# Output stages of a two-layer encoder trunk: another order of loads, additions and accumulators, and one gated row in steps

## The chip, the cores and the metric

The kernel runs on one core of a Trainium2 chip. A core has five engines, each of which works through its own list of instructions in order: TensorE (PE, the matrix multiplies, with its weight loads shown as PEld), VectorE (DVE), ScalarE (ACT), GpSimd (POOL) and SyncE (SP), which here only issues transfers (DMA). TensorE writes its sums into eight PSUM banks of 128 x 512 floats; everything else lives in SBUF tiles or in memory. The metric is the device time of one execution in microseconds (us).

## The reference

Inputs are x (1024 tokens x 1024 channels), 256 memory tokens and the weights of two layers. In each layer a normalised x goes through one wide input projection, several attentions work on its parts, their outputs are put side by side to 1536 channels, multiplied by a SiLU gate, and go through one output projection, which is added to x:

```
for l in range(DEPTH):
    h = rmsnorm(x, norm_gain[l])
    ...
    if l % 2 == 0:
        qa, ka, va, qb, kb, vb, qm, gate = split_cols(h @ w_in_even[e], SPLIT_EVEN)
        ...
        ya = global_gqa(...)
        yb = window_gqa(..., sink_b[e], rel_bias)
        ym = memory_attn(...)
        y = jnp.concatenate([ya, yb, ym], axis=-1) * jax.nn.silu(gate)
        x = x + y @ w_out_even[e]
    else:
        qc, kc, vc, qm, gate = split_cols(h @ w_in_odd[o], SPLIT_ODD)
        yc = neighborhood_attn(..., rpb_c[o])
        ym = memory_attn(...)
        y = jnp.concatenate([yc, ym], axis=-1) * jax.nn.silu(gate)
        x = x + y @ w_out_odd[o]
return rmsnorm(x, final_norm_gain)
```

The change concerns the lines `x = x + y @ w_out` of both layers and the gating of the last windowed heads of layer 0.

## The kernel before, in words

**Precision.** Every float32 operand of a product is split into a high part (rounded to the type that TensorE takes) and a low part (the rest). ACT makes the high part with a copy (L117), DVE or POOL the low part with a subtraction (L121 for operands, L1233 for weights). A product of two such operands is three matmuls: high by high, high by low, low by high.

**Who sets the order.** The program is written as if one instruction followed another. A planner then simulates the engines and gives every engine its own fixed list: of the instructions whose inputs and buffers it thinks ready, the one that comes first in the program goes first. `self.ahead(kind)` moves a group forward in that ranking by so many instructions (`AHEAD`, L35: in `out0` only the weights, `w`, by 300; in `out1` only `sink`, by 150). `issue_after(ins)` puts those instructions of a block that run on the engine of `ins` behind it. On the chip the lists are fixed: an instruction whose input is late holds up all that stand behind it on its engine. A tile's tag names a small set of buffers, which are used again as soon as the last reader of the old content is done; a load into a buffer still in use waits on SP.

**Layer 0 before its output stage.** `even` (L1824) runs four pairs of windowed heads, `window_pair` (L657), each in four groups g of 256 queries: scores on PE into `sa` banks, exponentials on ACT, scaling of the probabilities P on POOL (L702), transposes on PE (L125), their split on ACT and DVE (L526, L527), the product with the values on PE (L722) into the bank `pv`, and the close of the group (ACT copies half of `pv` to `bt`, DVE adds, L732). PE's waits in there are filled with other work from a list, `self.waiting`, of which `pull` takes some steps at given places: in the last pair (j = 3) these are the gates of rows 6 and 7 and the beginning of the output product (`begin_out`, L1240). When the gate of row 6 is complete, `gated_rows` writes all of its gating into the program at that one place (`gated`, L490): one multiply of 128 x 1024 on DVE (L499), a store of the result, a load of the partner row's halves back from memory, three subtractions of 128 x 512 on POOL (L510, L511, L513) and two more stores (L512, L514). Row 7, which needs the last group's result, follows after the pair (L1875).

**The output stage** (`out_project`, L1263) multiplies 12 row blocks of 128 gated channels. It is cut into two halves of channels, of tokens and of outputs, and uses seven half-size products in place of eight: a11, then t1 by s1, t2 by s2, t3 by s3, y22 by s4, y21 by a12 and t4 by a22. The t are sums and differences of the gated halves that the gating above stores in `yd`; the s are sums of weight blocks that `weight_sums` stores in `sd`. The channel blocks lie in the order `ROWS` (L44), so that row 6 is number 10 and row 7 number 11, the last one of a product. Each product has four output blocks i, each of 6 channel blocks x 3 = 18 matmuls of 128 x 512 (L1285), and takes two units of weights per block (192 KB each, loaded to `wraw`, split to `wh` and `wl`; four buffers of each). `y_parts` (L1176) loads the six operand blocks of a product (256 KB each, L1190) and splits them. A product's sum lies in a bank: `xb[i]` for a11 and, on top of it, t2 and t3; `yb[i]` for t1 and, on top of it, y22. `residual` (L1290) loads a block of x (256 KB, L1291) into the output tiles c11, c22, c12, c21, and `plus` (L1293, runs at L1294) adds a bank to it on DVE. `OUT` (L46) lists the tags of the operand and output tiles.

Before, the first two products stand in the program as: for each i the product a11, the load of c11's residual and the addition; then the six operand loads of t1; then for each i the weights of s1, the product, the load of c22's residual and the addition. In layer 0 the four `yb` banks are `tr[0]`, `pv`, `sa[0]` and `sa[1]`'s second halves, in this order; `pv` is the bank that the last windowed group still fills.

In layer 1 (`odd`, L1878; `near`, L1049) the gating already runs in steps, through `gated_steps` (L459), taken one at a time behind the scaling on POOL.

## Time and profile before

| what | us |
|---|---|
| median of 3 runs | 1513.12 |
| lowest and highest of them | 1510.55, 1514.97 |
| the profiled execution, its own time | 1518.44 |
| its span, first to last instruction | 1516.7 |
| PE busy in it | 1480.2 |
| granted TensorE clock, mean | 0.993 |

All times of the trace are us from the span's start. In a row of the timeline stand the start, the duration, the engine, the line, the operation, output<-inputs, the shapes, how many instructions were merged, and in brackets the idle time of the engine just before and what ended it. "SPq" is the issue of a transfer, not the transfer itself. A row of the waits reads: engine, tile and line that waited, what it waited for, the sum in us, how many times, the longest. In the view by windows, each engine's busy time is followed by the number of its instructions; then come the granted clock, the share of the DMA engines and their GB/s.

Layer 0's output stage runs from about 660 to 790 us of the span, layer 1's from about 1393 us to the end.

### The profile page before, as it was taken

The page shows a single profiled execution, that of the slowest core. Times are in us where ns is not written, and L with a number is a line of the kernel's source. Part 1 is how long each engine was busy: PE and PEld are TensorE (multiplying, and loading weights), DVE is VectorE, ACT ScalarE, POOL GpSimd, SP SyncE. Part 2 cuts the span into 40 slices and gives each one's busy share as a digit, 9 for nine tenths or more (in the row PEclk, how much of TensorE's full clock was granted, in tenths as well). Part 3 has the DMA queues.
Part 4 walks back from the last instruction along what each step waited for, and adds up shares of the span by engine and source line. Part 5 has one row for each costly group of instructions (what it writes and reads, how often), then busy time and mean ns, then how long its engine had stood idle before and what let it go on. Part 6 is the DMA issues. An engine that isn't in the chain of part 4 may idle for free.

```text
span 1516.7 us, 25292 instructions
## 1 busy us (share of the span) xinstructions
PE 1480.2 (98%) x8377; PEld 1272.6 (84%) x8377; DVE 1042.7 (69%) x2117; ACT 840.5 (55%) x1855; POOL 642.5 (42%) x766
## 2 busy tenths in 40 slices
PE   8999999999999999999999999999999999999997
PEld 8898897888888788887879877888898888888886
DVE  7686776777776667777577676654346777788754
ACT  7643664566656456655444444444346777778443
POOL 1323557746675645553450000002324555654455
PEclk9999999999999999999999999999999999999998
DMA  8956334334343524388653344567755577688833
GB/s 292 290 162 182 95 116 156 113 128 124 128 142 97 176 75 143 99 275 276 193 179 125 121 138 137 160 167 265 273 178 174 178 231 228 211 285 314 294 117 137
DMA packets 173859, 271.90 MB, mean 179 GB/s; under 512 B 15648, under 2 KB 96800, under 8 KB 172704
## 3 DMA queue, kind: packets, MB, share of 16 engines
q1 hardware_dynamic: 173296, 270.20, 55.2%
q8 instruction: 66, 1.08, 0.3%
q14 instruction: 65, 0.53, 0.1%
q10 hardware_dynamic: 432, 0.09, 0.0%
HBM read 174.28 MB, written 83.89 MB: 170 GB/s over the span
## 4 chain that ended last, share of the span: by engine, by line
PE 46%; DVE 4%; DMA 3%; issue 1%; ACT 1%; POOL 1%; SPq 0%; POOLq 0%; DVEq 0%; ACTq 0%
PE pj L62 10%; PE x L1532 6%; PE pj L1285 3%; PE pv L62 3%; PE y L1532 3%; PE sa L1285 3%; PE s L62 3%; PE s L1285 2%; PE tr L62 2%; PE tr L1285 2%; PE pv L1532 2%; PE pv L1285 2%; PE y L404 2%; PE pv L404 2%; DMA v<-vt 1%
## 5 line engine op out<-in xcount | busy, mean ns | idle before, releaser
L117 ACT ACTIVATE ph<-tr 128x512 fp32r<-128x512 f32 (+2 forms) x336 | 180.9, 540 | 123.1 <-PE tr L125 82.3
L527 DVE TENSOR_TENSOR pl<-tr,ph 128x512 fp32r<-128x512 f32 (+2 forms) x336 | 205.5, 614 | 55.2 <-ACT ph L117 54.2
L231 PE MATMUL pj<-H,wh 128*128 128x512 f32 x704 | 235.4, 414 | 0.5 <-DVE vt L302 0.2
L147 POOL TENSOR_SCALAR wh<-wraw 128x512 fp32r<-128x512 f32 x48 | 31.8, 665 | 271.3 <-PE x L1532 236.6
L117 ACT ACTIVATE wh<-wraw 128x384 fp32r<-128x384 f32 (+1 forms) x163 | 89.2, 553 | 102.4 <-PE tr L1285 13.5
L231 PE MATMUL pj<-H,wl 128*128 128x512 f32 x352 | 139.6, 397 | 0.0
L231 PEld LDWEIGHTS pj<-H,wh 128*128 128x128 f32 x704 | 120.6, 190 | 18.8 <-POOL wl L149 0.6
L62 PE MATMUL pj<-H,wh 128*128 128x512 f32 x384 | 121.4, 397 | 0.0
L125 PE MATMUL tr<-ident,P 128*128 128x128 f32 x752 | 117.5, 273 | 3.8 <-POOL P L702 1.3
L1084 POOL TENSOR_SCALAR pn<-pn,st 128x384 f32<-128x384 f32 (+1 forms) x128 | 75.2, 588 | 99.7 <-DVE st L1083 60.8
L1233 POOL TENSOR_TENSOR wl<-wraw,wh 128x384 fp32r<-128x384 f32 x56 | 64.1, 1146 | 114.4 <-ACT wh L117 80.4
L125 PEld LDWEIGHTS tr<-ident,P 128*128 128x128 f32 x752 | 89.1, 140 | 13.9 <-POOL P L702 2.6
L1005 ACT ACTIVATE P<-sa,st 128x1024 f32<-128x1024 f32 x64 | 71.6, 1118 | 45.2 <-DVE st L1004 25.4
L1082 ACT ACTIVATE pn<-pn,st 128x384 f32<-128x384 f32 (+1 forms) x128 | 75.1, 587 | 35.4 <-DVE st L1079 33.0
L1007 POOL TENSOR_SCALAR P<-P,st 128x1024 f32<-128x1024 f32 x64 | 74.3, 1164 | 33.7 <-DVE st L1006 28.9
L1004 DVE TENSOR_REDUCE st<-sa 128x1 f32<-128x1024 f32 x64 | 77.6, 1218 | 14.2 <-PE sa L1000 11.3
L62 PE MATMUL s<-k,q 128*128 128x384 f32 (+1 forms) x352 | 86.4, 341 | 0.0
L149 POOL TENSOR_TENSOR wl<-wraw,wh 128x512 fp32r<-128x512 f32 x52 | 68.2, 1313 | 27.0 <-ACT wh L117 24.1
L231 PEld LDWEIGHTS pj<-H,wl 128*128 128x128 f32 x352 | 66.4, 189 | 15.2
L62 PE MATMUL pj<-H,wl 128*128 128x512 f32 x192 | 75.8, 395 | 0.0
L821 PE MATMUL pj<-ah,H 128*128 128x256 f32 x384 | 72.5, 287 | 1.4 <-DVE H L766 1.3
L62 PEld LDWEIGHTS pj<-H,wh 128*128 128x128 f32 x384 | 66.7, 189 | 5.5
(503 smaller groups left out, 4200.6 us busy)
## 6 DMA issues: line engine op xcount, KB each, us to landing
wraw<-w_o SPq DMA_DIRECT2D x52, 256.0 KB, 3.9
y<-yb SPq DMA_DIRECT2D x24, 512.0 KB, 3.3
wraw<-s SPq DMA_DIRECT2D x64, 192.0 KB, 3.3
wraw<-w_e SPq DMA_DIRECT2D x44, 256.0 KB, 3.3
k<-k SPq DMA_DIRECT2D x42, 256.0 KB, 4.3
s<-bias SPq DMA_DIRECT2D x56, 192.0 KB, 2.0
y<-sg SPq DMA_DIRECT2D x20, 512.0 KB, 3.9
wq<-w_o SPq DMA_DIRECT2D x40, 256.0 KB, 3.6
```

Of the source, the lines that this page charges most:

```text
L62: return lambda *a, **k: self.tc.keep_in_program_order(getattr(self.engine, name)(*a, **k))
L117: return self.nc.scalar.activation(out, in_, AF.Copy, scale=scale)
L125: self.turned = self.fence = self.pe.transpose(o, i, self.ident)
L231: self.pe.matmul(a[:, :n], s[:, kt % UNIT, :], m, start=(kt == 0 and i == 0), stop=(kt == KT - 1 and i == 2))
L527: self.low = nc.vector.tensor_tensor(pl[:, :n], tr[:, :n], ph[:, :n], op=OP.subtract)
L821: self.last = nc.tensor.matmul(a[:, b * 256:(b + 1) * 256], x[kt][:, t], w, start=(kt + b + i == 0), stop=(kt == KT - 1 and i == 2), skip_ ...
L1004: nc.vector.tensor_reduce(st[:, 0:1], s, axis=AX.X, op=OP.max, negate=True)
L1007: self.normal = nc.gpsimd.tensor_scalar(pt, pt, st[:, 2:3], 0.5, op0=OP.mult, op1=OP.mult)
L1082: nc.scalar.activation(o, o, AF.Exp, bias=st[:, 0:1], scale=-1.0, accum_out=st[:, 2:3])
L1084: normal = nc.gpsimd.tensor_scalar(o, o, st[:, 3:4], 0.5, op0=OP.mult, op1=OP.mult)
L1285: last = nc.tensor.matmul(bank, s[:, k, :], y[3 * u + k][m][:, cols], start=start and u + k + e == 0, stop=u == 1 and k + e == 4, skip_gro ...
L1532: self.last = nc.tensor.matmul(bank, ws[s][:, k, :], b[k][m], start=start and k + i == 0, stop=k == UNIT - 1 and i == 2, skip_group_check= ...
```

## The change

Four edits in one:

1. In `out_project` the four a11 products stand alone. Behind them come the two weight units of s1 for i = 0, then t1's operand loads, with the weights of i = 1 put in ahead of the fifth of the six (`between`), then for each i the t1 product, and only then the residual load and addition of c11 and those of c22. This holds for both layers.
2. In layer 0 the `yb` banks come in the order `tr[0]`, `sa[0]`, `sa[1]`, `pv`.
3. Row 6 of layer 0 is gated through `gated_steps` instead of `gated_rows`: the multiply in two halves of 512, and the POOL subtractions and stores as steps.
4. `window_pair` takes one step (`later_job`) at each transposing round, its POOL part behind the group's last scaling; what is left over is taken after the pair.

```
@@ out_project
             if i >= begun:
                 with self.tc.issue_after(self.hold.ins) if self.hold else nullcontext():
                     product(first, xb[i], weights(i, "a11") if i > begun else self.early, True)
+
+        ready = [list(weights(0, "s1"))]
+        y = self.y_parts(yd, tags["y"][1], "t1", lambda: ready.append(list(weights(1, "s1"))))
+        for i in range(4):
+            product(y, yb[i], weights(i, "s1") if i > 1 else ready[i], True)
             residual(at(c11, i), i, 1)
             with self.ahead("sink"):
                 plus(at(c11, i), xb[i])
-
-        y = self.y_parts(yd, tags["y"][1], "t1")
-        for i in range(4):
-            product(y, yb[i], weights(i, "s1"), True)
             residual(at(c22, i), 4 + i, 2)
             with self.ahead("sink"):
                 plus(at(c22, i), yb[i])
@@ y_parts
-    def y_parts(self, yd, tags, kind):
+    def y_parts(self, yd, tags, kind, between=None):
...
+            if k == 4 and between:
+                between()
@@ build, layer 0
-                y = [tr[0], self.ps("pv"), sa[0][:, 1, :], sa[1][:, 1, :]]
+                y = [tr[0], sa[0][:, 1, :], sa[1][:, 1, :], self.ps("pv")]
@@ even, j == 3
-                self.lazily(lambda: self.gate(w, E_G + 6), lambda sg: self.gated_rows(sg, 6, y6, yd))
+                self.later_jobs = deque()
+                self.lazily(lambda: self.gate(w, E_G + 6),
+                            lambda sg: self.later_jobs.append(self.gated_steps(sg, y6, yd, ROWS.index(6))))
@@ even, after the pairs
+        while self.later_jobs:
+            deque(self.later_jobs.popleft(), 0)
         self.gated_rows(sgs[0], 7, y, yd)
...
+    def later_job(self, normal):
+
+        if self.later_jobs:
+            with self.tc.issue_after(normal.ins):
+                if next(self.later_jobs[0], self) is self:
+                    self.later_jobs.popleft()
@@ window_pair
             for t in range(0, len(todo), 2):
+                self.later_job(normal)
```

More of the change, by code (lines that the diff above doesn't have):

```diff
@@ L84, in __init__ @@
         self.pe, self.ready, self.due = self.nc.tensor, {}, 0
+        self.later_jobs = ()
     def ahead(self, kind):
```

## The prediction

> **What bounds the kernel now.** I read the page first: who is busy, and how much of the span is left over.

> ```profile
> span 1516.7 us, 25292 instructions
> PE 1480.2 (98%) x8377; PEld 1272.6 (84%) x8377; DVE 1042.7 (69%) x2117; ACT 840.5 (55%) x1855; POOL 642.5 (42%) x766
> ```

> PE is busy for all but 36.5 us, and the change takes no matmul away. So it can gain no more than the idle time of PE in the stages that it reorders, and only where nothing later takes it back. Next I read the view by windows for both output stages, and kept the windows in which PE has idle time (the first PE figure is its busy time in 10 us):

> ```profile
> 650.00:660.00 10.00, 8.94 (x54) 7.56 (x53) 7.85 (x18) 5.57 (x14) 6.82 (x7) 1.00 0.98 353
> ...
> 680.00:690.00 10.00, 7.58 (x34) 5.76 (x33) 5.81 (x10) 4.58 (x9) 1.09 (x1) 1.00 0.77 261
> ...
> 710.00:720.00 10.00, 9.69 (x41) 7.14 (x40) 8.01 (x13) 7.40 (x15) 2.45 (x2) 1.00 0.89 325
> ...
> 790.00:800.00 10.00, 8.23 (x51) 6.73 (x49) 6.79 (x20) 3.80 (x7) 1.17 (x1) 1.00 0.81 267
> ...
> 1390.00:1400.00 10.00, 8.71 (x42) 6.78 (x40) 9.90 (x18) 9.95 (x21) 1.01 (x1) 1.00 0.70 237
> ```

> That is 1.06 + 2.42 + 0.31 + 1.77 + 1.29 = 6.9 us. The 1.77 at 790 us follow the last sums of squares, which no edit touches; 5.1 us are in reach. Last, PE's timeline, only the rows in which it stood idle, and the place where its next work lay:

> ```profile
> 656.81 1.11 PE L125 MATMUL tr<-ident,P 128*128 128x128 f32 x5 [0.94 <-POOL P L702]
> ...
> 684.64 0.28 PE L722 MATMUL pv<-pl,v 128*128 128x256 f32 x1
> 686.97 0.73 PE L1285 MATMUL sa<-q,wh 128*128 128x512 f32 x2 [2.05 <-ACT wh L117]
> 688.07 0.51 PE L1285 MATMUL sa<-q,wl 128*128 128x512 f32 x1 [0.36 <-DVE wl L1233]
> ...
> 719.58 0.50 PE L1285 MATMUL pj<-H,wl 128*128 128x512 f32 x1 [0.31 <-DVE wl L1233]
> ...
> 1392.88 0.44 PE L62 MATMUL pv<-pl,v 128*128 128x384 f32 x1 [1.15 <-DVE pl L527]
> ```

> **Row 6 in steps: 0.94 us.** The wait at 656.81 is for the scaling of a group's probabilities, and POOL's timeline says why that was late:

> ```profile
> 651.62 1.29 POOL L510 TENSOR_TENSOR sg<-yb,sg 128x512 f32<-128x512 f32 x1 [3.27 <-DMA sg<-y]
> 652.88 1.74 POOL L511 TENSOR_TENSOR sg<-yb,sg 128x512 f32<-128x512 f32 x1
> 654.58 1.31 POOL L513 TENSOR_TENSOR yb<-sg,yb 128x512 f32<-128x512 f32 x1
> 655.85 2.59 POOL L702 TENSOR_SCALAR P<-P,st 128x384 f32<-128x384 f32 x4
> ```

> POOL first waits 3.27 us for row 6's partner to come back from memory, then does the three subtractions (1.29 + 1.74 + 1.31 = 4.3), and the scaling stands behind them. Its reciprocal was done well before:

> ```profile
> 653.99 0.16 DVE L697 RECIPROCAL st<-st 128x4 f32<-128x4 f32 x1
> ```

> At 654.15 the scaling could have started, 1.70 us sooner. With seven steps, one for each of three transposing rounds in groups 1 to 3, the partner's load falls into group 1, the first two subtractions behind group 2's scaling, the third behind group 3's. Both waits leave that place, and 0.94 us of PE's idle time goes. What the steps add: two multiplies of 512 in place of one of 1024 on DVE, and nothing on SP (the same five transfers). The subtractions now run beside group 3's scaling, for which there is a row:

> ```profile
> 663.69 4.27 POOL L702 TENSOR_SCALAR P<-P,st 128x384 f32<-128x384 f32 x4
> ...
> 668.42 2.10 DVE L121 TENSOR_TENSOR k<-k 128x512 fp32r<-128x512 f32 x2
> ```

> The same four scalings took 4.27 us here against 2.59 above, while DVE split operands. The moved subtractions can cost up to that difference, 1.68 us, on group 3, or nothing. I take nothing, since PE has no idle row between 656.81 and 686.97: a11 covers it. Should the cover be gone, it is 1.68.

> [...]

> **The order of accumulators, and weights and operands first: 2.41 us.** Before the gap at 684.9 us PE has done 12 of the 18 matmuls of t1's block 0; the last 6 need operands in the tile v, which the windowed heads hold until PE's last `pv` matmul at 684.64. The next block in the program is block 1, but its bank is `pv`, closed only here:

> ```profile
> 687.46 0.59 ACT L117 ACTIVATE bt<-pv 64x512 f32<-64x512 f32 x1
> ...
> 688.54 0.84 DVE L732 TENSOR_TENSOR yb<-pv,bt 64x256 f32<-64x256 f32 x2
> ```

> So the list of PE has block 2 (`sa`) first, with weights that come last, and ACT holds them behind operands of y22, whose loads took 6 us:

> ```profile
> 679.27 0.52 ACT L117 ACTIVATE wh<-wraw 128x384 fp32r<-128x384 f32 x1 [2.17 <-PE tr L1285]
> 684.18 0.63 ACT L117 ACTIVATE q<-q 128x512 fp32r<-128x512 f32 x1 [4.39 <-DMA q<-y]
> 684.72 0.51 ACT L117 ACTIVATE wh<-wraw 128x384 fp32r<-128x384 f32 x1
> ...
> 686.41 0.51 ACT L117 ACTIVATE wh<-wraw 128x384 fp32r<-128x384 f32 x1
> ```

> The chain of waits gives what a matmul takes when nothing holds it, 8.40 / 36 = 0.233 us:

> ```profile
> 1393.60 8.40 PE s L1285 x36
> ```

> With `sa[0]` as block 1's bank nothing is open: its first unit of weights is the one split at 679.27, ready when PE gets there at 684.9; its 9 matmuls last until 687.0, and the second unit (684.72) is ready by then; the third (686.41) follows. So both waits, 2.05 + 0.36, go. If y22's operands still stand ahead of the second unit and come later, up to all 2.41 stays. I take 2.41, because the edit takes away the bank that forced block 2 forward. The 0.31 at 719.58 has the same kind of cause (a weight unit behind operands on ACT and DVE); I count it as gone, between 0 and 0.31.

> What the reordering moves: 4 residual loads and 4 additions of c11 go past t1's 6 operand loads and up to 8 weight units on SP, and past their splits on DVE. No instruction is added. The loads before (source line 1291 in layer 0; issue in ns, then us to landing):

> ```profile
> L1291 SPq DMA_DIRECT2D P<-xT x12: 327/368/493, 648.8 to 676.7; - x12
> ...
> DMA to landing us min/median/max: 2.8/5.1/6.3
> ```

> An addition must be done before t2 writes on the same bank (`xb`). t1's 72 matmuls, 16.8 us, lie between; the load, 5.1 at the median, and the addition, 0.69 (the row of 1391.06 below), are covered by them.

> **Layer 1: 0.60 us.** DVE's timeline ahead of 1392.88:

> ```profile
> 1391.06 0.69 DVE L1294 TENSOR_TENSOR H<-H,pj 128x512 f32<-128x512 f32 x1
> 1391.66 0.69 DVE L467 TENSOR_TENSOR yb<-yb,mk 128x512 f32<-128x512 f32 x1
> 1392.28 0.88 DVE L527 TENSOR_TENSOR pl<-tr,ph 128x384 fp32r<-128x384 f32 x2
> ```

> The addition to c11 stands ahead of the split that PE waits for. Moved behind t1's products it frees 0.60 us (1391.06 to 1391.66); the bounds are 0 (`sink` still pulls it 150 places forward) and 1.15. PE has no other wait in that stage before its end, so nothing more can be won there.

> **The sum.** 0.94 + 2.41 + 0.31 + 0.60 = 4.26 us. The profiled execution took 1518.44, so it would take 1514.2. It lay 5.3 above the median of the three runs; on the median's scale, 1513.12 - 4.26 = **1508.9 us**. A measurement of this kernel can tell about 0.3% (4.5 us) from no change; the forecast lies almost on that bound.

> **Rivals.**

> *Given back at row 11.* t2's last operand is row 7's gated block (number 11). Its store and PE's first matmul with it, the 16th of block 0:

> ```profile
> 700.10 0.38 SPq L512 DMA_DIRECT2D y<-sg  x1
> ...
> 710.38 0.69 DVE L121 TENSOR_TENSOR H<-H 128x512 fp32r<-128x512 f32 x1 [0.24 <-ACT H L117]
> ...
> 711.15 0.40 PE L1285 MATMUL pj<-H,wh 128*128 128x512 f32 x1
> ```

> Split until 711.07, used at 711.15: no slack. If PE comes 2.41 sooner and this chain doesn't, PE waits here. Against it: the chain begins with the close of `pv`, which itself stood behind y22's splits on ACT from 684.9 to 687.46 and may move up as much. Kept would be 0.94 + 0.60: 1511.6.

> *More than the sum.* A new plan also shifts the other stages, which hold 36.5 - 6.9 = 29.6 us of idle time. A tenth of that on top: 1513.12 - 4.26 - 3.0 = 1505.9. For it speaks that such waits are many and small; against it, that nothing there is edited.

> *Slower: residual loads in front of row 7.* Before, SP issues the residuals early, into a time when nothing waits:

> ```profile
> 648.84 3.07 SPq L1291 DMA_DIRECT2D P<-xT  x4
> ```

> After, 8 of them (c11 and c22) follow t1's operands in the program, the last two of which wait for v:

> ```profile
> 686.83 0.38 SPq L1190 DMA_DIRECT2D v<-y  x1
> ...
> 691.26 0.32 SPq L508 DMA_DIRECT2D y<-yb  x1
> ```

> If they land between these two rows, 8 x 0.262 MB = 2.1 MB stand ahead of row 7's store and its partner's load. At the 353 GB/s of the window 650 to 660 that is 5.9 us, and 8 issues of 0.37 us (368 ns above) are up to 3.0 more. Row 11 has no slack, so t2 waits for all of it, and of the sum only 0.94 + 0.60 stays: 1517.5 to 1520.5, 1519 in the middle. It decides from about 6 loads on. Against it: the planner lets a ready load go past one that waits for a buffer, as y22's loads did here.

> *It doesn't do what it says.* Weights already rank 300 places forward; with the same lists in the end, 1513.1.

> **How the numbers follow.** Forecast 0.40, its own range 1506 to 1511 (all 5.1 us in reach and one replanned wait below; the 2.41 half closed and 0.9 of the contention above); 0.26 of it beyond the bound, 0.14 within. More than the sum 0.17, faster. Given back 0.12 and unchanged 0.05, both within. Slower 0.26. So faster 0.43, the same 0.31, slower 0.26. The range reaches to the far ends of both side cases, 1502 (the larger gain, less another 4 us of replanned waits) to 1520.

> **What would show it.** Right: no PE row with an idle time of 2 us between 680 and 692; block 1 of t1 in `sa` directly behind block 0; no POOL subtraction ahead of group 2's scaling; the addition of c11 behind the last window split in layer 1. Wrong: PE idle at t2's 16th matmul (given back), or SP rows of L1291 between the v loads and L508 with a later L512 (slower). A difference that lies outside 650 to 800 and 1380 to 1400 us would make the account wrong even where the time fits.

## The result, and the profile after

The changed kernel took 1516.76 us in the median of its runs, the kernel before 1511.97 us beside it on the same chip: a ratio of 1.0028 with a 95% interval of 1.0017 to 1.0039. The prediction was 1508.9 us, a gain of 4.26; the change lost about 4.8. The profiled execution took 1519.19 us, and its page differs little from the one before: PE has 1481.1 us of work and stands idle for 36.3 us, where it was 1480.2 and 36.5. Of all the runs here, one, of the two-edit kernel in the third session below, took 1795.22 us at a clock of 0.75; it is left out of every figure.

```profile
span 1517.4 us, 25283 instructions
PE 1481.1 (98%) x8377; PEld 1271.7 (84%) x8377; DVE 1041.5 (69%) x2118; ACT 840.0 (55%) x1855; POOL 640.6 (42%) x766
```

So the idle time that the change was to remove is still there, in other places. PE's timeline of the changed kernel, with only the rows in which it stood idle at the places of the prediction, the row ahead of the largest and the row behind the last wait of t1:

```profile
636.55 0.44 PE L683 MATMUL sa<-k,q 128*128 128x384 f32 x1 [0.48 <-DVE st L687]
637.55 0.44 PE L683 MATMUL sa<-k,q 128*128 128x384 f32 x1 [0.40 <-DVE st L687]
...
687.12 0.40 PE L1289 MATMUL sa<-k,wl 128*128 128x512 f32 x1
689.32 0.86 PE L1289 MATMUL sa<-q,wh 128*128 128x512 f32 x2 [1.80 <-ACT wh L118]
690.52 0.80 PE L1289 MATMUL tr<-v,wh 128*128 128x512 f32 x1 [0.34 <-ACT v L118]
...
692.57 0.79 PE L1289 MATMUL sa<-q,wl 128*128 128x512 f32 x1 [0.83 <-DVE wl L1237]
693.16 1.05 PE L1289 MATMUL sa<-q,wh 128*128 128x512 f32 x2
...
1394.05 0.44 PE L62 MATMUL pv<-pl,v 128*128 128x384 f32 x1 [1.15 <-DVE pl L528]
```

The line numbers are 1 to 5 higher than before (L1289 was L1285, L118 was L117, L1237 was L1233, L528 was L527). The wait of 0.94 us for POOL at 656.81 has gone, but 0.48 + 0.40 = 0.88 us stand ahead of it. The wait of 2.05 + 0.36 = 2.41 us at 685 has become 1.80 + 0.34 + 0.83 = 2.97 us at 687 to 692.6. The 0.31 us at 719 has gone. The 1.15 us of layer 1 is as it was. Together 0.94 + 2.41 + 0.31 = 3.66 us became 3.85: +0.2.

That is no explanation of 4.8 us. The row at 693.16 points to something else: two matmuls took 1.05 us, where a pair of the same form takes 0.62 to 0.64 elsewhere. The view by windows, cut where the granted clock changes, says why (PE's busy time is the first figure behind the length, the granted clock the third from the end):

```profile
686.38:689.79 3.41, 1.61 (x7) 0.87 (x6) 3.04 (x5) 3.39 (x7) 0.00 (x0) 1.00 1.04 399
689.79:693.20 3.41, 2.25 (x6) 1.04 (x5) 3.41 (x6) 1.56 (x3) 1.14 (x1) 0.50 0.77 250
693.20:696.62 3.42, 3.42 (x10) 2.65 (x9) 1.65 (x3) 0.52 (x1) 1.86 (x2) 0.50 0.80 281
696.62:700.03 3.41, 3.41 (x17) 2.81 (x16) 2.90 (x3) 1.09 (x3) 2.23 (x2) 1.00 0.38 127
```

PE was idle for 3.41 - 1.61 = 1.80 us of the first window. In the next two its clock was 0.50, and in the last of those, busy throughout, it began 10 matmuls where the window behind it has 17. Cut in the same way, the execution before had its idle time at this place spread over two such windows, and no fall:

```profile
682.48:685.90 3.42, 2.43 (x11) 1.72 (x10) 0.69 (x1) 1.70 (x4) 0.60 (x1) 1.00 0.94 329
685.90:689.31 3.41, 1.98 (x7) 1.35 (x8) 3.39 (x6) 2.65 (x5) 0.49 (x1) 1.00 0.45 152
689.31:692.72 3.41, 3.41 (x16) 2.77 (x15) 3.38 (x5) 2.03 (x4) 1.73 (x1) 1.00 0.63 212
```

It had falls elsewhere, at 61, 150, 235 and 1099 us, each behind a wait of 1.1 to 2.9 us; the changed kernel's execution had them at 235 and 1099. So both profiled executions have four such stretches (both also end at half clock, behind 1508 and 1512 us, as every profile here does). Whether a given wait is followed by a fall differs from one profiled execution to another: the 1.83 us at 150 us stand in all 14 profiles here, with a fall behind them in six. The profiled execution of the kernel before, 1518.44 us, lay 6.5 us above that kernel's median, the changed one's 2.4 above its own. So two profiled spans, 1516.7 and 1517.4 us, can lie 0.7 us apart while the medians lie 4.8 apart.

### The profile page after: what moved, and what is told of

Read it like the earlier page. It is cut to its first block, busy times and chain, and to the rows that moved or that the text cites. A ratio compares the mean times of both kernels' runs of the same rounds, so it can differ in the third digit from the quotient of the medians.

```text
span 1517.4 us, 25283 instructions
## 1 busy us (share of the span) xinstructions
PE 1481.1 (98%) x8377; PEld 1271.7 (84%) x8377; DVE 1041.5 (69%) x2118; ACT 840.0 (55%) x1855; POOL 640.6 (42%) x766
## 4 chain that ended last, share of the span: by engine, by line
PE 78%; DMA 8%; DVE 6%; issue 3%; POOL 3%; ACT 2%; SPq 1%; POOLq 0%; DVEq 0%; ACTq 0%
PE pj L232 14%; PE pj L62 10%; PE x L1537 6%; PE tr L126 5%; PE pj L1289 4%; PE sa L1289 3%; PE pv L1034 3%; PE y L1537 3%; PE pv L62 3%; PE s L62 3%; PE s L1289 2%; PE tr L1289 2%; PE tr L62 2%; PE pv L1537 2%; PE sa L1001 2%
## 5 line engine op out<-in xcount | busy, mean ns | idle before, releaser
L118 ACT ACTIVATE ph<-tr 128x512 fp32r<-128x512 f32 (+2 forms) x336 | 180.9, 540 | 121.4 <-PE tr L126 80.1
L528 DVE TENSOR_TENSOR pl<-tr,ph 128x512 fp32r<-128x512 f32 (+2 forms) x336 | 205.5, 615 | 58.1 <-ACT ph L118 57.1
L118 ACT ACTIVATE wh<-wraw 128x384 fp32r<-128x384 f32 (+1 forms) x163 | 88.9, 552 | 97.1 <-PE pj L1289 12.8
L232 PEld LDWEIGHTS pj<-H,wh 128*128 128x128 f32 x704 | 120.1, 190 | 18.7 <-POOL wh L148 0.6
L62 PE MATMUL pj<-H,wh 128*128 128x512 f32 x384 | 121.4, 397 | 0.0
L126 PE MATMUL tr<-ident,P 128*128 128x128 f32 x752 | 116.5, 273 | 1.9 <-POOL P L641 1.2
L1237 POOL TENSOR_TENSOR wl<-wraw,wh 128x384 fp32r<-128x384 f32 x56 | 62.0, 1110 | 118.1 <-ACT wh L118 99.5
L126 PEld LDWEIGHTS tr<-ident,P 128*128 128x128 f32 x752 | 89.0, 140 | 11.3 <-POOL P L641 2.6
L62 PE MATMUL s<-k,q 128*128 128x384 f32 (+1 forms) x352 | 86.3, 341 | 0.0
L62 PE MATMUL pj<-H,wl 128*128 128x512 f32 x192 | 75.8, 395 | 0.0
L1237 DVE TENSOR_TENSOR wl<-wraw,wh 128x384 fp32r<-128x384 f32 (+1 forms) x67 | 51.3, 766 | 29.6 <-ACT wh L118 29.5
```

The source lines that it names most:

```text
L62: return lambda *a, **k: self.tc.keep_in_program_order(getattr(self.engine, name)(*a, **k))
L118: return self.nc.scalar.activation(out, in_, AF.Copy, scale=scale)
L126: self.turned = self.fence = self.pe.transpose(o, i, self.ident)
L232: self.pe.matmul(a[:, :n], s[:, kt % UNIT, :], m, start=(kt == 0 and i == 0), stop=(kt == KT - 1 and i == 2))
L528: self.low = nc.vector.tensor_tensor(pl[:, :n], tr[:, :n], ph[:, :n], op=OP.subtract)
L1237: engine.tensor_tensor(lf, raw, hf, op=OP.subtract)
```

## The experiments

Each run lists the mean granted clock, so a kernel's mean clock is the mean over its runs. The product of span and clock of a run is roughly its length at the full clock (roughly, because the product counts the clock also where TensorE stands idle). Over some 12 runs the difference of two such means is known to about 1.4 us; the changed kernel's third time has only 6 runs, and there it is about 2.5. "Clock" and "full-clock length" below are these two means, the latter as the difference to the kernel before in the same session. The kernel before ran in every session, the changed kernel in the second and third; "the steps" are edits 3 and 4.

| kernel | median us | ratio to before, 95% | clock (before's) | full-clock length |
|---|---|---|---|---|
| edit 1 undone | 1513.64 | 0.9998 [0.9982, 1.0014] | 0.9963 (0.9958) | +1.2 |
| edit 1 alone | 1514.78 | 1.0002 [0.9987, 1.0018] | 0.9959 (0.9958) | +0.4 |
| changed, y22's splits held | 1511.68 | 1.0004 [0.9983, 1.0025] | 0.9965 (0.9958) | +1.6 |
| before, y22's splits held | 1512.19 | 1.0004 [0.9987, 1.0020] | 0.9956 (0.9958) | 0.0 |
| changed, second time | 1515.13 | 1.0024 [1.0005, 1.0043] | 0.9941 (0.9958) | +0.4 |
| changed, wait filled | 1512.43 | 0.9998 [0.9988, 1.0009] | 0.9962 (0.9958) | +0.1 |
| edits 1 and 2 | 1512.29 | 0.9997 [0.9983, 1.0010] | 0.9955 (0.9958) | -1.3 |
| edit 1 and the steps | 1515.93 | 1.0019 [1.0003, 1.0034] | 0.9952 (0.9958) | +1.8 |
| changed, third time | 1517.97 | 1.0045 [1.0027, 1.0062] | 0.9937 (0.9960) | +2.3 |
| changed, filled elsewhere | 1516.47 | 1.0029 [1.0017, 1.0041] | 0.9945 (0.9960) | +1.9 |
| edits 1 and 2, second time | 1511.24 | 0.9999 [0.9986, 1.0011] | 0.9958 (0.9960) | -0.8 |
| edits 1 and 2, wait in t1 filled, seven matmuls more at 150 us | 1511.71 | 1.0005 [0.9994, 1.0016] | 0.9969 (0.9960) | +1.5 |

**First session: which part, and is it the operands of y22?** Theory A took the loss for edit 1's: the loads of y22 go out late, their splits hold the weights on ACT, PE waits and then has half its clock. Theory B put it on row 6 in steps, theory C on chance. The first kernel is the changed one with the order of the first two products as before, the second the kernel before with edit 1 alone.

> The changed kernel without its first edit (a11's additions, t1's operands and weights in the order of before), with the other order of accumulators and row 6 in steps. Theory A: the loss comes from the first edit, which sends residual loads just ahead of y22's operand loads; y22's splits then come late on ACT (first at 686.05 after 684.18) and hold the weights of t1's block 2, so PE idles 1.80 + 0.34 + 0.83 us at 687 to 693 and then runs 6.83 us at half clock. Then this kernel is not slower than before: ratio to before 0.998 to 1.000. Theory B: the loss comes from row 6 in steps (the last scores of the windowed heads lie at 660.8 instead of 659.4). Then it stays slow: ratio 1.002 to 1.004. Theory C: the clock falls by chance and the plan costs only 0.6 us more idle time: ratio about 1.000.

> The kernel before with the first edit alone (order of loads, weights and additions in both output stages; accumulators and row 6 as before). Theory A: about as slow as the whole change, ratio to before 1.002 to 1.004, with the wait for weights in t1 and the fall of the clock behind it. Theory B: no slower than before, 0.999 to 1.001. Theory C: about 1.000.

Edit 1 undone gave 0.9998 and edit 1 alone 1.0002. A expected 1.002 to 1.004 for edit 1 alone and fails as the account of the whole loss; B expected that for the kernel without edit 1 and fails too. Neither part has the loss by itself. C, chance, expected about 1.000 for both and isn't refuted by these runs.

In the other two kernels the splits of y22's operands in layer 0 may not be issued before the last weight split of s1, so nothing of y22 stands ahead of t1's weights:

```
-        self.copy(hf, raw)
-        engine.tensor_tensor(lf, raw, hf, op=OP.subtract)
+        self.w_last = self.copy(hf, raw), engine.tensor_tensor(lf, raw, hf, op=OP.subtract)
...
+        behind = self.w_last
...
+        held = self.held
+        if not last:
+            self.held = behind
         y = self.y_parts(yd, tags["y"][4], "y22")
+        self.held = held
```

> The changed kernel, with the splits of y22's operands in layer 0 put behind the last weight split of s1 on ACT and on the engine of its low part; nothing else is touched. Theory A: the weights of t1's block 2 are split at about 685, PE's waits in t1 go, and so does the half clock: ratio to before 0.996 to 0.999, to the changed kernel 0.993 to 0.997. Theory B: still slower than before, 1.001 to 1.003. Theory C: 0.6 to 3 us less than the changed kernel, 1.000 to 1.002 to before.

> The kernel before with the same hold on y22's splits. Theory A: the 2.05 + 0.36 us wait at 685 to 688 goes or shrinks to the wait for the weight buffer (under 1 us): ratio to before 0.997 to 1.000. If the wait in the kernel before comes from the bank of the last windowed group instead, it stays: 1.000.

The held kernel before gave 1.0004: no difference. In its profile the wait at 685 is gone, but one of 1.91 us stands at 697.56, with a fall behind it. The held changed kernel gave 1.0004 too. Its interval, up to 1.0025, still reaches the loss of 1.0024 to 1.0045 measured elsewhere, so that it is without the loss is likely and not shown; it gains nothing against the kernel before, where A had 0.996 to 0.999. Its profile was the surprise. PE's timeline has more waiting there than the changed kernel's 2.97 us:

```profile
685.24 0.50 PE L1288 MATMUL tr<-v,wh 128*128 128x512 f32 x1 [1.56 <-ACT v L118]
...
694.07 0.50 PE L1288 MATMUL pv<-k,wl 128*128 128x512 f32 x1 [1.20 <-POOL wl L1236]
...
698.31 0.50 PE L1288 MATMUL pj<-H,wl 128*128 128x512 f32 x1 [1.44 <-DVE wl L1236]
```

That is 4.2 us, but in three pieces some 4 to 9 us apart, and the clock did not fall. So the sum of the waits may not be what sets the time; how close together they lie might. From here theory H says: the changed kernel's wait in t1 is concentrated enough that TensorE's clock falls behind it in most executions, and that is the loss.

**Second session: the clock, by filling the wait.** The rivals were P (the plan itself is longer, at the same clock) and I (chance). The changed kernel ran again, and then with seven matmuls of t1's own operands put into the wait. They compute nothing that is kept.

```
             product(y, yb[i], weights(i, "s1") if i > 1 else ready[i], True)
+            if i == 1 and not last:
+                with self.tc.issue_after(self.mid.ins):
+                    for _ in range(7):
+                        nc.tensor.matmul(yb[i + 1], ready[i][0][0][:, 0, :], y[0][0], start=True, stop=True, skip_group_check=True)
```

(`self.mid` is the twelfth matmul of the block.)

> The changed kernel once more, beside before on the same chip. Theory H (half clock): the wait in t1 (layer 0) lies within about 5 us now (1.80 + 0.34 + 0.83 us), so that the granted clock falls there in most executions; the median ratio is 1.002 to 1.004, the mean granted clock of its runs is 0.001 to 0.003 below that of before's runs, and span times clock agrees with before's within 1 us. Theory P (the plan itself is longer, by waits and later work): 1.002 to 1.004 with the same mean clock, span times clock 3 us or more longer. Theory I (the difference was chance, or that chip's): 0.999 to 1.001.

> The changed kernel with seven matmuls of t1's own operands (0.234 us each, 1.64 us) issued behind block 1's first twelve matmuls in layer 0, into block 2's accumulator, which the block's first matmul overwrites: the wait stays as it is, but TensorE isn't idle in it. Theory H: the clock no longer falls near 690 us, the mean clock of its runs is 0.001 to 0.002 above that of the unfilled kernel on this chip, and the ratio to before is 0.998 to 1.001, that is 0.001 to 0.003 under the unfilled one. Theory P: as the unfilled kernel or slower, 1.002 to 1.005. Theory I: 0.999 to 1.002, as the unfilled one.

The changed kernel gave 1.0024 at a clock of 0.9941 against 0.9958, and the full-clock lengths lie 0.4 us apart. With that C falls as well. Filled, it gave 0.9998 at 0.9962. That is 2.7 us faster in the median, with seven matmuls more. H named both in advance; P and I fail. PE's timeline of the filled kernel shows that the wait is still there:

```profile
688.46 1.79 PE L1326 MATMUL sa<-q,wh 128*128 128x512 f32 x7
691.06 0.73 PE L1289 MATMUL sa<-q,wh 128*128 128x512 f32 x2 [0.81 <-ACT wh L118]
692.17 0.50 PE L1289 MATMUL tr<-v,wh 128*128 128x512 f32 x1 [0.38 <-ACT v L118]
...
693.50 0.50 PE L1289 MATMUL sa<-q,wl 128*128 128x512 f32 x1 [0.60 <-DVE wl L1237]
```

1.79 us of filling and 0.81 + 0.38 + 0.60 us of idle time make 3.58 us, no less than 2.97. But its windows have no idle time above 1.29 us, and the clock stays at 1.00:

```profile
687.33:690.75 3.42, 2.92 (x13) 2.04 (x11) 2.26 (x5) 2.95 (x6) 0.00 (x0) 1.00 1.06 402
690.75:694.16 3.41, 2.12 (x7) 1.17 (x8) 3.41 (x5) 2.42 (x5) 0.90 (x1) 1.00 0.71 239
694.16:697.57 3.41, 3.29 (x15) 2.39 (x14) 2.37 (x4) 0.53 (x1) 0.72 (x2) 1.00 0.94 334
```

The price can be read from the stage. From PE's last `pv` matmul of the windowed heads to its first matmul of t2 the filled execution took 702.55 - 682.77 = 19.78 us; the changed kernel's took 703.02 - 681.65 = 21.37 and 701.67 - 680.12 = 21.55, each with two stretches at half clock, and 700.79 - 680.17 = 20.62 in the third session, with one.

In the same session ran the changed kernel without the steps (edits 1 and 2 alone) and without the new accumulators (edit 1 and the steps):

> The changed order of the first output stage and of the accumulators, but row 6 gated as before. Theory H: the same wait in t1 as in the changed kernel, so 1.001 to 1.004 and a mean clock 0.001 to 0.002 under before's; if the wait falls apart into pieces under 1.5 us, 0.999 to 1.001 and before's clock. Theory P, row 6 in steps being the cost: 0.997 to 1.000; the two orders being the cost: 1.002 to 1.004 with the same clock. Theory I: 0.999 to 1.001.

> The changed order of the first output stage and row 6 in steps, accumulators as before. Theory H: the second product's block waits for the last window's two addends on pv in one piece of about 2 us (1.98 us in the kernel with the order alone), so the clock falls there in about half of the executions: 1.000 to 1.002, clock 0 to 0.001 under before's. Theory P, accumulators being the cost: 0.998 to 1.000; else 1.002 to 1.004. Theory I: 0.999 to 1.001.

Without the new accumulators, block 1 waits for `pv`'s bank and operands in one piece, and the kernel is slower, 1.0019, with a fall behind it. H had put the wait at 2 us and the ratio at 1.000 to 1.002. Of its 2.8 us in the mean, though, 1.8 are full-clock length and only 1.0 is clock:

```profile
685.64 0.70 PE L1289 MATMUL pv<-q,wh 128*128 128x512 f32 x2 [3.13 <-ACT k L118]
```

Without the steps there is no loss, 0.9997, as H allowed for a wait in pieces. Its PE rows at the two places:

```profile
652.90 1.11 PE L126 MATMUL tr<-ident,P 128*128 128x128 f32 x5 [0.82 <-POOL P L703]
...
683.50 0.40 PE L1289 MATMUL sa<-k,wl 128*128 128x512 f32 x1
683.74 0.73 PE L1289 MATMUL sa<-q,wh 128*128 128x512 f32 x2
684.83 0.50 PE L1289 MATMUL tr<-v,wh 128*128 128x512 f32 x1 [0.36 <-ACT v L118]
...
686.97 0.59 PE L1289 MATMUL sa<-q,wl 128*128 128x512 f32 x1 [1.42 <-DVE wl L1237]
```

Block 2's high weights are there when block 1's twelve matmuls end (683.50 + 0.23). The two orders without the steps have 0.36 + 1.42 = 1.78 us of waiting in t1, the changed kernel 2.97. The clock fell behind it in this profile too, for one stretch, and so it did at this place in the profiles of edit 1 alone (682.50) and of edits 1 and 2 the second time (684.56), which show no loss. So a fall in t1 is not the changed kernel's alone; what its profiles have and these don't is, in two of three, a second stretch. The wait of 2.05 us in the kernel before can be followed by a fall too, by the counts of the last section; one profile of a kernel can't tell how often.

**Third session: is it the place of the filling?** Theory F held that seven more matmuls anywhere re-plan the stage. The control puts the same seven ahead of block 1 of the sixth product (y21), behind t1; the order of the matmuls up to there is the changed kernel's.

```
             parts = list(weights(i, "a12"))
+            if i == 1 and not last:
+                for _ in range(7):
+                    nc.tensor.matmul(xb[i], parts[0][0][:, 0, :], y[0][0], start=True, stop=True, skip_group_check=True)
```

> The changed kernel a third time, as the reference of this call. Theory H (half clock): 1.001 to 1.004, mean clock 0.001 to 0.003 below before's; in the profile the wait in t1 of layer 0 leaves TensorE idle for more than 1.7 us of one stretch of 3.41 us and the granted clock falls to 0.50 behind it, for two stretches. Theory F (the filled kernel was faster because its schedule came out another way, not by the clock): the same ratio.

> The changed kernel with the same seven matmuls (0.234 us each, 1.64 us) issued ahead of the second block of the sixth product (y21, layer 0), some 80 us behind the wait in t1, into an accumulator that the block's first matmul overwrites; the order of all other matmuls is the changed kernel's. Theory H: the clock falls in t1 as in the changed kernel, and the seven matmuls cost up to 1.64 us: 1.002 to 1.005, clock 0.001 to 0.003 below before's. Theory F (seven matmuls more, anywhere, re-plan the stage): 0.999 to 1.001.

Filled elsewhere: 1.0029 at a clock of 0.9945 against 0.9960; the changed kernel beside it 1.0045 at 0.9937. F fails. The control's windows show the fall, two stretches again:

```profile
682.82:686.23 3.41, 0.90 (x4) 0.38 (x2) 2.49 (x5) 3.17 (x7) 0.00 (x0) 1.00 1.05 400
686.23:689.64 3.41, 2.48 (x5) 1.09 (x5) 3.41 (x5) 2.11 (x5) 1.17 (x1) 0.52 0.68 221
689.64:693.06 3.42, 3.42 (x8) 2.72 (x9) 1.67 (x3) 0.52 (x1) 1.31 (x2) 0.50 0.90 308
```

The last two kernels were to beat both: the two orders without the steps, and the same with the wait in t1 filled and with seven matmuls meant for a wait of 1.83 us ahead of layer 0's first scores, which all 14 profiles have.

```
+                if not self.filled:
+                    self.filled = True
+                    for _ in range(7):
+                        nc.tensor.matmul(s[:, 0:512], self.h[0][0][:, 0:128], self.h[0][0][:, 0:512], start=True, stop=True, skip_group_check=True)
                 for c in range(0, T, 512):
```

> The two changed orders without row 6 in steps, again, as the reference of the next kernel. Theory H: the wait in t1 in two pieces, 0.998 to 1.001, clock within 0.001 of before's. Theory F: the same.

> The two changed orders without row 6 in steps, with seven matmuls (0.234 us each) into the wait of t1 in layer 0, and seven of resident operands into the wait of 1.83 us ahead of layer 0's first scores (about 148 us), which all profiles so far show and behind which the clock fell in four of ten. Theory H: no stretch at half clock at 150 or 690 us, mean clock 0.001 to 0.002 above that of the two edits alone, 0.9975 to 1.0000: faster than both kernels, if by little. Theory F: 0.999 to 1.002, as the two edits alone or slower.

The clock rose as H expected, 0.9969 against 0.9958, and neither place fell in the profile. But the kernel gained nothing by it: 1.0005, against 0.9999 for the unfilled one. H's 0.9975 to 1.0000 is missed, and F's 0.999 to 1.002 holds. The trace says why this is no test of filling two waits. In t1 the filling took the whole wait: PE has no idle row there. At 150 us it did not:

```profile
149.54 1.89 PE L1003 MATMUL sa<-H 128*128 128x512 f32 x7 [1.83 <-DVE q L122]
```

The seven matmuls began behind the wait, which is as long as before, and added their own length. That the clock didn't fall there owes nothing to them: the grid of stretches (last section) happened to cut the idle time there into 0.31 and 1.52 us. So of the fourteen matmuls, 3.3 us at 0.234 us each, half are pure cost; the full-clock length is 2.3 us above the unfilled one's. No version beat the kernel before by more than the interval.

## Why the prediction was wrong

**Where the time went.** In the second session the changed kernel's mean time was 1516.07 us, 3.02 above that of before; 0.4 of this is full-clock length, 2.7 is clock. The clock is 0.0017 lower, which over 1517 us is 1517 x 0.0017 / 0.5 = 5.2 us more at half clock per execution, or 1.5 stretches of 3.41 us. The profiles show such stretches where the change works: all four of the unfilled kernel's schedule (three of the changed kernel, one of the control) have half clock in t1, three of them for two stretches; the one profile of the kernel before has none there. In the third session the full-clock length is 2.3 us longer as well (six runs; 1.9 in the control, 1.6 of whose matmuls were added). That is more than the +0.2 of the idle times, and this part stays open. The table hints at one cause: the kernels with the steps stand at +0.1 to +2.3 in the last column, those without, nothing added, at -1.3 to +0.4. So the steps may cost something beside the clock; no run was made to test it.

**The order of accumulators and weights first, 2.41: the step that failed.** "So both waits, 2.05 + 0.36, go" was half right. Block 1 does run in `sa` directly behind block 0, as foretold, but the next thing is late: block 2's weights. The prediction named this bound ("if y22's operands still stand ahead of the second unit and come later, up to all 2.41 stays") and took the other end: of the third unit of weights it says that it "follows", at no cost. It was split at 686.41 before and is split at 688.76 now, 1.41 us after PE had come to the end of what it could do (687.12 + 0.23). So 2.41 us of waiting did not go but became 2.97. SP and ACT of the changed kernel show it:

```profile
673.46 0.32 SPq L489 DMA_DIRECT2D y<-yb  x1
...
675.81 0.85 SPq L1295 DMA_DIRECT2D yb<-xT  x2
676.72 0.90 SPq L1295 DMA_DIRECT2D P<-xT  x2
...
679.34 0.91 SPq L1295 DMA_DIRECT2D P<-xT  x2
...
680.82 0.85 SPq L1194 DMA_DIRECT2D q<-y  x2
```

```profile
686.05 0.63 ACT L118 ACTIVATE q<-q 128x512 fp32r<-128x512 f32 x1 [4.33 <-DMA q<-y]
686.70 0.60 ACT L118 ACTIVATE bt<-pv 64x512 f32<-64x512 f32 x1
687.20 0.62 ACT L118 ACTIVATE q<-q 128x512 fp32r<-128x512 f32 x1
687.72 1.14 ACT L118 ACTIVATE k<-k 128x512 fp32r<-128x512 f32 x2
688.76 0.51 ACT L118 ACTIVATE wh<-wraw 128x384 fp32r<-128x384 f32 x1
```

ACT sat idle for 4.33 us in front of y22's first operand, with the weights behind it in its list. On DVE the low half came later still, behind the gating of row 7 and two more splits:

```profile
688.82 1.22 DVE L500 TENSOR_TENSOR yb<-yb,sg 128x1024 f32<-128x1024 f32 x1
689.95 1.29 DVE L122 TENSOR_TENSOR k<-k 128x512 fp32r<-128x512 f32 x2
691.16 1.35 DVE L1237 TENSOR_TENSOR wl<-wraw,wh 128x384 fp32r<-128x384 f32 x1
```

**Why the parts matter together.** The operand chain is what PE meets, and the steps move it. In the changed kernel y22's first load goes out at 680.82, 3.75 us before block 1 begins (684.57). In the kernel without the steps it goes out 6.67 us before (674.27 against 680.94), behind four residual loads and not six:

```profile
652.43 0.72 SPq L515 DMA_DIRECT2D y<-yb  x1
...
658.49 0.91 SPq L1295 DMA_DIRECT2D yb<-xT  x2
...
670.88 1.46 SPq L1295 DMA_DIRECT2D P<-xT  x3
...
672.87 0.42 SPq L1295 DMA_DIRECT2D P<-xT  x1
...
674.27 0.33 SPq L1194 DMA_DIRECT2D q<-y  x1
```

The two more go into `yb`. Without the steps they went out at 658.49, some 16 us ahead of y22's first load; with the steps only at 675.81, 5 us ahead of it. All eight profiles with the steps have them 4.3 to 5.2 us ahead, all six without 15.7 to 16.4. The reading is that row 6, gated in steps, gives its `yb` back late: its last store (`y<-yb`, L489 or L515) goes out at 673.46, without the steps at 652.43, and the loads wait for it. The prediction had the steps add "nothing on SP (the same five transfers)"; they are the same five, but later. That these two loads alone hold up y22's isn't shown: no run tried it alone. With the splits on ACT and DVE the same distance behind the close of the last group in both kernels (wh 2.06 us behind `bt`: 688.76 - 686.70, and 683.18 - 681.12 without the steps), PE comes to block 2 some 2 us sooner in the changed one (0.65 us behind `bt`, 2.62 without the steps), and waits.

**Row 6 in steps, 0.94.** Right where it was looked for: no PE wait at 656.81, no POOL subtraction ahead of group 2's scaling, and no contention that reached PE. Wrong in the sum: the new plan pays 0.88 of it back a group earlier. DVE does the reciprocal of a group's sums at 637.41 instead of 635.46, behind the next group's evictions, and PE waits for these to free the score banks. First the kernel before, then the changed one:

```profile
635.46 0.18 DVE L697 RECIPROCAL st<-st 128x4 f32<-128x4 f32 x1 [0.78 <-ACT P L695]
```

```profile
633.24 0.69 DVE L468 TENSOR_TENSOR yb<-yb,sg 128x512 f32<-128x512 f32 x1
...
637.41 0.17 DVE L698 RECIPROCAL st<-st 128x4 f32<-128x4 f32 x1
```

The rows 0.48 and 0.39 or 0.40 (L683) stand in the profiles of all eight kernels with the steps and in none of the six without them, which have 0.81 to 1.27 us of waits for POOL's scaling (L125 or L126) from 628 to 662 us, in three rows each. The 0.69 us multiplication of the first step is what came ahead; that it moved the reciprocal is argued and not shown. One reading of the prediction was off here: the DVE row that it shows with the 4.27 us scaling, at 668.42, begins 0.46 us after that scaling's end. The splits that did run beside it took 0.68 to 0.99 us each. The 0.9 us of contention in the prediction's range is shown by no run: in the changed kernel's profile group 3's scaling takes 3.83 us, where it took 4.27, and the three moved subtractions 1.29 to 1.31 us each.

**The 0.31 at 719** was won as counted. **The 0.60 of layer 1** was not: the addition to c11 is still ahead of the split that PE waits for (DVE at 1392.22, the split at 1393.45), and PE's wait is 1.15 us before and after. That was the lower bound of 0, whose reason in the prediction was that the additions still rank 150 places forward.

**The rivals.** Row 11 gave nothing back: PE has no wait there, and row 7's stores go out earlier than before (L513 at 698.15; 700.10 before). The residual loads did not come ahead of row 7, but ahead of y22's operands. So the mechanism of the slower rival, loads let past on SP, was near, and its victim and price were not.

**The missing term.** Nothing in the sum or in the rivals let a wait cost more than its own length. The kernel before had the rows for it, the granted clock of 0.50 behind four waits of 1.1 to 2.9 us; they were read as a mean clock of 0.993 and no more. The signs that were to show the prediction right could not tell either: three of the four hold (no idle row of 2 us between 680 and 692, where the longest is now 1.80; block 1 in `sa`; no subtraction ahead of group 2's scaling), and the first of them passes over three waits under 2 us that add up to 2.97. The waits of 0.88 us at 637 lie outside the stretches that the prediction named.

## What to carry to other kernels

Where a mean granted clock is under 1, cut the view by windows at its changes first: here 1.80 us of idle time in one window were followed by 6.83 us at a clock of 0.50, while 1.56 + 1.20 + 1.44 us, some 4 to 9 us apart in the held changed kernel, were followed by no fall. So ask how the waits lie, and not only for their sum. Where a wait is filled with other work, look in the trace whether the work lies in the wait or behind it. When a bank or an order stops binding, ask what the next block needs and who holds that in its list; here it was another product's operands on ACT, which waited 4.33 us for a transfer. A gain that ends in front of a chain fed by transfers can be idled away there: here 2.41 us of waiting became 2.97, and in the profile 6.83 us at half clock came on top.

## What the runs showed of the hardware

The first session's kernel before shows what this is worth without any change: of its 35 runs the two with a clock of 0.998 took 1508.9 us in the mean and the four with 0.994 took 1515.6. A run's mean clock also holds the half clock at its end, 4.8 to 8.3 us of the span in the 14 profiles.
